# A two-layer trunk on one core: reordering the end of the attention, with 18 output-projection products inside it

## The chip, the cores and the metric

The kernel runs on one core of a Trainium2 chip. The metric is device time in microseconds (us) of one execution; a comparison takes medians of several executions.

## The reference

The model has two layers over 128 context tokens and 512 latent tokens of width 1024. Layer 0 is gated grouped-query attention (16 heads of 64, 4 key/value heads), layer 1 a gated linear recurrence in both directions (8 heads of 128). Each layer ends in a product with an output matrix, a gate and a LayerNorm. What the change touches is layer 0 from the softmax to its norm:

```python
s = jnp.einsum('bqkgd,bskd->bkgqs', q_blk, kf) * scale
p = jax.nn.softmax(s, axis=-1)
o = jnp.einsum('bkgqs,bskd->bqkgd', p, vf)
...
gated = o.reshape(B, L, ATTN_WIDTH) * jax.nn.silu(g)
out = gated @ w_out
x = _layer_norm(DEEPNORM_ALPHA * x + gate * out, ln_gain, ln_bias)
```

Latent tokens read the 128 cached context keys and all 512 latent keys; context tokens read the context alone.

## The kernel before, in words

All matrix products keep full precision by splitting each fp32 operand into a high and a low part (hi, lo) and adding three products: hi·hi, hi·lo, lo·hi. A weight piece of 128x1024 is loaded into a buffer `raw`, cast by ScalarE into its high part (L232), and VectorE subtracts to get the low part (L233). `raw` has three buffers, so a load for a later piece is issued by SyncE when VectorE has finished the subtraction of the piece three places before it. The order of the pieces is fixed: the eight pieces of the attention's output matrix (`in_attn_w_out`: four for output columns 0 to 511, `nh` = 0, then four for `nh` = 1), then those of the recurrence's input matrix (`in_rec_w_in`).

**Attention.** The work is a list of 36 units, nine for each of the four key/value heads (`att_gen`, L976). A sample unit is one head against 256 latent queries, as two blocks of 128. For each block there is a *front* (L927): four products of scores `sc` on TensorE (L838, L839), the row maximum on VectorE (`nm`, L932), the exponential on ScalarE (`p`, L935, with the row sum read out after it), the reciprocal on VectorE (`rc`, L939) and the scaling of the probabilities on GpSimd (`p`, L940). Then come ten transposes of the two blocks' probabilities (`pt`, L947) and their copies into SBUF (`pts`, L843: two by ScalarE, one by VectorE). Two heads make a pair, and when both are transposed the pair's value products follow (`pot`, L865; ten per pair, each of which the trace counts as two instructions); VectorE multiplies the result by the gate path (`gs`, L870). The code issues fronts two units ahead. All of this, with the projections of the next queries, stands in one block that is ordered by a scheduler (`first_half`, a simulated timeline); an instruction that is wrapped in `pin` keeps its place in program order on its engine. Before the change the scores, transposes and value products aren't pinned.

The gated output `gs` is split into `hhi` and `hlo` (L1063, L1064), eight column groups k = 0 to 7. The groups 0 to 5 belong to the first three key/value heads and are split while the last head is still at work; groups 6 and 7 are split at the end. The last four pieces of the output matrix (`nh` = 1) go into memory that the attention has used, so ScalarE can cast them only when the last value product is done.

**Output projection and norm, layer 0** (second block, from L1202). For each tile `tt` of 128 tokens and each `nh`, 24 products of 128x512 (three for each k) make `outp` (L1112 to L1114). VectorE multiplies by the gate, adds the scaled residual, and takes the statistics (L1128 to L1130, in `Norm.half`); after both `nh`, `Norm.finish` aggregates, GpSimd takes the power -1/2, and VectorE normalises `y` in two halves (L1141). The normalised tile is then transposed (`h1t`, L1208, in `h1_tile`) to become input of layer 1. The order is (tt, nh) = (0,0), (1,0), (0,1), (1,1), then the first transposes `h1t` of tile 0, then (2,0), (2,1), `h1t` of tile 1 and so on. Between the parts the first two pieces of `in_rec_w_in` are cast and subtracted (`rhi`, `rlo`).

**PSUM.** During the attention it is three pools: `b2` (two double banks, scores), `pop` (one bank, value products), `b1` (three banks, transposes and others). `Phase(4, 0)` replaces them by four double banks. Before the change it is opened inside the first block.

**Order on an engine.** Each engine runs its own instructions strictly in order; an instruction that waits holds all behind it on that engine.

Of the kernel before, what the change touches and what calls it, by code (L numbers as in the profile page):

```python
# [11 lines left out]
F32 = mybir.dt.float32  # L12
# [3 lines left out]
ALU = mybir.AluOpType  # L16
AX = mybir.AxisListType

P = 128
D = 1024  # L20
KT = D // P
# [3 lines left out]
CW = 256  # L25
NH = 16
NKV = 4
HD = 64
# [8 lines left out]
LEAD = (1, 1)  # L37
RAW_START = 8
EARLY = 2
WARM = (8, 2, 3)  # L40
D_SCALE = 2
D_OUTS = 2
# [83 lines left out]
def drain(gen):  # L126
    for _ in gen:
        pass
# [3 lines left out]
def hybrid_step(ctx: ExitStack, tc: tile.TileContext, a: dict, o: dict):  # L132
# [3 lines left out]
    def pool(name, bufs, **kw):  # L136
        return tc.tile_pool(name=name, bufs=bufs, **kw)
# [15 lines left out]
    class Phase:  # L153
        def __init__(self, n2, n1):
            self.st = ExitStack()
            if n2:
                pools["b2"] = self.st.enter_context(pool("b2", n2, space=PSUM))
            pools.pop("b1", None)
            if n1:
                pools["b1"] = self.st.enter_context(pool("b1", n1, space=PSUM))  # L160
# [673 lines left out]
                        next(att)  # L834


    def score_mms(out, X, c, h, t0, k0, k1):
        nc.tensor.matmul(out, X[:, h, t0:t0 + P], kk[:, c, k0:k1], start=True, stop=False)  # L838
        nc.tensor.matmul(out, X[:, h, t0:t0 + P], klo[:, c, k0:k1], start=False, stop=True)  # L839

    def keep_pt(ps, w, eng):
        t = sm.tile([P, w], F32, tag=f"pt{w}", name="pts", bufs={512: 6, 256: 4}[w])
# [11 lines left out]
    def tick():  # L854
        due = [f for f in later if f[0] <= 1]
        later[:] = [f for f in later if f[0] > 1]
        for f in later:
            f[0] -= 1
        for _, fn in due:
            fn()  # L860

    def av_mms(pot, slot, c, moving, first, last):

        for j in (1, 0):
            nc.tensor.matmul(pot[j * HD:(j + 1) * HD, :CW], vv[:, slot, c * HD:(c + 1) * HD], moving[j], start=first, stop=last)  # L865

    def av_out(pot, gt):
        tv = pot[:, :CW]
# [54 lines left out]
    def sample_unit(c, h, qh):  # L923
        j = h % 2
        ps, pts = {}, {}

        def front(i):  # L927
            sc = bank2("sc")
            for n, (k0, k1) in enumerate(HALVES):
                score_mms(sc[:, n, :320], Xs[c], c, h, (2 * qh + i) * P, k0, k1)  # L930
            nm = tiny.tile([P, 4], F32, tag="nm", name="nm")
            nc.vector.tensor_reduce(nm[:, 0:1], sc[:, :, :320], AX.XY, ALU.max, negate=True)  # L932
            p = ps[i] = prob_tile("p")
            su = tiny.tile([P, 4], F32, tag="su", name="su")
            nc.scalar.activation(halves(p[:]), sc[:, :, :320], AF.Exp, bias=nm[:, 0:1], accum_out=su[:, 0:1])  # L935

            def scale():
                rs = tiny.tile([P, 4], F32, tag="rc", name="rc")
                nc.vector.reciprocal(rs[:, 0:1], su[:, 0:1])  # L939
                nc.gpsimd.tensor_scalar(p, p, rs[:, 0:1], 1.0, ALU.mult, ALU.mult)  # L940
            defer(D_SCALE, scale)

        def trans(k0, m):
            pt = bank1("pt")
            for i in range(m):
                for q in range(2):
                    nc.tensor.transpose(pt[:, i * 256 + q * P:i * 256 + (q + 1) * P],  # L947
                                        ps[q][:, (k0 + i) * P:(k0 + i + 1) * P], ident)
            pts[k0] = keep_pt(pt, m * 256, nc.scalar.copy if m == 2 else nc.vector.tensor_copy)
            for i in range(m):  # L950
                live[j, k0 + i] = pts[k0][:, i * 256:(i + 1) * 256]

        def pair():
            mine = {k: live.pop(k) for k in list(live)}

            def apply():
                pot = pop[0].tile([P, 512], F32, tag="po", name="pot")
                for n, k in enumerate((4, 0, 1, 2, 3)):
                    av_mms(pot, k, c, [mine[0, k], mine[1, k]], n == 0, n == 4)
                av_out(pot, gs[:, 2 * c + h // 2, qh * 256:(qh + 1) * 256])  # L960
            return apply

        return (c, [lambda: front(0), lambda: front(1)], [lambda: trans(0, 2), lambda: trans(2, 2), lambda: trans(4, 1)],
                pair if j else None)

    def att_gen(side):
        units = []
        for c in range(4):
            units += [sample_unit(c, j, qh) for qh in range(2) for j in range(2)] + [prompt_unit(c)]
            units += [sample_unit(c, 2 + j, qh) for qh in range(2) for j in range(2)]  # L970
        AHEAD = 2

# [12 lines left out]
        for u in range(AHEAD):  # L985
            for f in fronts(u):
                run(f)
                yield
        pending = []

        def flush():
            while pending:
                run(pending.pop(0))
                yield

        for u, (c, _, back, end) in enumerate(units):
# [12 lines left out]
            back_of[0] = c  # L1009
            if end:  # L1010
                pending.append(end if len(back) == 2 else end())
        yield from flush()
        while later:
            tick()

    side = Side()
    att = att_gen(side)
# [32 lines left out]
        return modA, modB  # L1050

    wo = {}

    def wo_gen(layer, pieces, wpool):
        for nh, i in pieces:
# [36 lines left out]
    right.close()  # L1092


    ph = Phase(4, 0)
    h1p = rpool("h1p", 1)
    h1lo = h1p.tile([P, KT, NT], F32R, tag="h1lo", name="h1lo")
    wr = rpool("wr", 2)
# [8 lines left out]
    def out_mms(ps, tt, nh, ghi, glo, ks=range(KT), c=slice(0, 512)):  # L1107
        t = slice(tt * P, (tt + 1) * P)
        out = bank_of(ps, nh, c)
        for k in ks:  # L1110
            hi, lo = (w[:, k % 2, c] for w in wo[nh, k // 2])
            nc.tensor.matmul(out, ghi[:, k, t], hi, start=(k == 0), stop=False)  # L1112
            nc.tensor.matmul(out, ghi[:, k, t], lo, start=False, stop=False)  # L1113
            nc.tensor.matmul(out, glo[:, k, t], hi, start=False, stop=(k == KT - 1))  # L1114

    class Norm:
# [7 lines left out]
        def half(self, nh):  # L1124
            s = slice(nh * 512, (nh + 1) * 512)
            y = self.y[:, s]
            g = gate[0][:, 1 if self.tt == TS else 0, s]
            nc.vector.tensor_tensor(y, self.ps[:, nh, :], g, ALU.mult)  # L1128
            nc.vector.scalar_tensor_tensor(y, self.x[:, s], ALPHA, y, ALU.mult, ALU.add)
            nc.vector.bn_stats(self.st[:, nh, :], y)  # L1130

# [68 lines left out]
    drain(split_gs(range(6, 8)))  # L1200
    drain(wo_gen(0, PIECES[4:], wob))
    first_half.__exit__(None, None, None)  # L1202
    h1hi = gsp.tile([P, KT, NT], F32R, tag="gs", name="h1hi")
    def h1_tile(tt, y):
        s = 1 if tt == TS else 0
        pt = bank2("h1t")
        for ft in range(KT):
            nc.tensor.transpose(pt[:, ft // 4, (ft % 4) * P:(ft % 4 + 1) * P], y[:, ft * P:(ft + 1) * P], ident)  # L1208
        t = slice(tt * P, (tt + 1) * P)
        for nh in range(2):  # L1210
            h = lnp.tile([P, 512], F32, tag="h", name="h1", bufs=2)
            for f in range(4):
                ft = 4 * nh + f
                src, dst = pt[:, nh, f * P:(f + 1) * P], h[:, f * P:(f + 1) * P]
                ma, mb = modA[:, ft, s:s + 1], modB[:, ft, s:s + 1]
                if f % 2:
                    nc.scalar.activation(dst, src, AF.Identity, bias=mb, scale=ma)
                else:
                    nc.vector.tensor_scalar(dst, src, ma, mb, ALU.mult, ALU.add)
            f = slice(4 * nh, 4 * nh + 4)  # L1220
            split_act(h1hi[:, f, t], h1lo[:, f, t], h[:].rearrange("p (a b) -> p a b", a=4))
# [116 lines left out]
    first = proj_gen(0, H, True)  # L1338
    next(first)
    norms = {}  # L1340
    for tt, nh in ((0, 0), (1, 0), (0, 1), (1, 1), (2, 0), (2, 1), (3, 0), (3, 1), (4, 0), (4, 1)):
        if nh == 0:
            norms[tt] = Norm(tt)
        out_mms(norms[tt].ps, tt, nh, hhi, hlo)
        norms[tt].half(nh)
        if nh == 1:
            norms[tt].finish()
            if tt > 1:
                h1_tile(tt - 1, norms[tt - 1].y)
            elif tt == 1:  # L1350
                h1_tile(0, norms[0].y)
    for _ in range(4):
        next(first)
    h1_tile(TS, norms[TS].y)
# [373 lines left out]
```

## Time and profile before

| | |
|---|---|
| median of 3 runs | 844.93 us (841.62 to 847.22) |
| the profiled execution | 845.85 us, of which the span of the profile is 844.1 us |
| TensorE busy | 817.6 us, 97% of the span |
| VectorE, ScalarE, GpSimd busy | 531.3, 383.3, 211.5 us |
| mean granted clock of TensorE | 0.989 |
| last value product of the attention ends | 337.2 us |
| first output-projection product starts | 337.73 us |
| first transposes `h1t` start | 359.67 us |

A row of the timeline reads: start, duration, engine, line and operation, out<-in and shape, count, and in brackets how long the engine had been idle before it and what ended that. A matmul's listed duration overlaps the next one's; the pace is the distance between starts. PEclk is the clock that TensorE was granted, as a share of full speed. In a chain row the number is the time that the chain spends there.

### The profile page before, as it was taken

How to read it: one execution, taken by the hardware profiler on the slowest of the kernel's cores; microseconds unless marked ns; L12 is line 12 of the kernel's file. 1: busy time of each engine (PE TensorE's matmuls, PEld its weight loads, DVE VectorE, ACT ScalarE, POOL GpSimd, SP SyncE). 2: the span in 40 equal slices, each digit the busy share in tenths (PEclk: the TensorE clock that was granted, in tenths of full speed). 3: DMA queues.
4: the chain of work that ended last, by engine and by line, in shares of the span. 5: the costliest groups of instructions: out<-in, count | busy, mean ns of one | idle time of the engine just before them, and what ended most of it. 6: DMA issues, size and time to landing. Idle time of an engine off the chain costs nothing.

```text
span 844.1 us, 19415 instructions
## 1 busy us (share of the span) xinstructions
PE 817.6 (97%) x8157; PEld 732.2 (87%) x8157; DVE 531.3 (63%) x954; ACT 383.3 (45%) x771; POOL 211.5 (25%) x263
## 2 busy tenths in 40 slices
PE   8999998999999998999999999999999999999994
PEld 6789998878789765888999999999999999998774
DVE  4566434675756665776438575767668575858476
ACT  2242536474756765322434434445434544445232
POOL 0123002343334752110001304143333314121121
PEclk9999999999999999999999999999999999999997
DMA  9932212144151153631322322331422322324041
GB/s 333 384 114 76 78 49 77 51 142 166 54 203 51 51 200 101 218 131 36 106 71 63 106 73 84 83 108 52 107 89 83 91 68 89 120 64 158 21 162 75
DMA packets 34134, 92.50 MB, mean 110 GB/s; under 512 B 5040, under 2 KB 12224, under 8 KB 34048
## 3 DMA queue, kind: packets, MB, share of 16 engines
q1 hardware_dynamic: 23280, 73.05, 25.8%
q0 software_dynamic: 4864, 14.44, 5.8%
q10 hardware_dynamic: 5904, 3.78, 1.5%
q8 instruction: 64, 1.05, 0.5%
q14 instruction: 22, 0.18, 0.1%
HBM read 82.06 MB, written 9.19 MB: 108 GB/s over the span
## 4 chain that ended last, share of the span: by engine, by line
PE 88%; DVE 5%; ACT 2%; DMA 2%; issue 1%; POOL 0%; SPq 0%; DVEq 0%; ACTq 0%; POOLq 0%
PE rps L1273 7%; PE rps L1274 7%; PE rps L1275 7%; PE vgps L1263 5%; PE vgps L1265 5%; PE vgps L1264 5%; PE pot L865 4%; PE outp L1112 4%; PE pt L947 3%; PE outp L1114 3%; PE outp L1113 3%; PE acc L523 3%; PE lv L1406 2%; PE gps L338 2%; PE gps L339 2%; PE sc L838 2%
## 5 line engine op out<-in xcount | busy, mean ns | idle before, releaser
L1273 PE MATMUL rps<-h1hi,rhi 128*128 128x320 f32 x368 | 118.3, 321 | 0.0
L1274 PE MATMUL rps<-h1lo,rhi 128*128 128x320 f32 x368 | 113.8, 309 | 0.0
L1275 PE MATMUL rps<-h1hi,rlo 128*128 128x320 f32 x368 | 113.6, 309 | 0.0
L940 POOL TENSOR_SCALAR p<-p,rc 128x640 f32<-128x640 f32 x64 | 54.1, 847 | 124.7 <-DVE rc L939 108.7
L932 DVE TENSOR_REDUCE nm<-sc 128x1 f32<-128x640 f32 x64 | 52.1, 819 | 33.6 <-PE sc L839 33.0
L1273 PEld LDWEIGHTS rps<-h1hi,rhi 128*128 128x128 f32 x368 | 69.1, 188 | 1.3
L1274 PEld LDWEIGHTS rps<-h1lo,rhi 128*128 128x128 f32 x368 | 69.2, 188 | 0.0
L1275 PEld LDWEIGHTS rps<-h1hi,rlo 128*128 128x128 f32 x368 | 69.1, 188 | 0.0
L233 DVE TENSOR_TENSOR rlo<-raw,rhi 128x1024 fp32r<-128x1024 f32 x32 | 45.0, 1407 | 34.1 <-ACT rhi L232 34.0
L1434 POOL COPY At<-near 32x160 f32<-32x160 f32 x32 | 14.0, 438 | 196.0 <-DVE near L1396 195.0
L935 ACT ACTIVATE p<-sc,nm 128x640 f32<-128x640 f32 x64 | 51.3, 803 | 23.3 <-DVE nm L932 12.9
L232 ACT CAST rhi<-raw 128x1024 fp32r<-128x1024 f32 x32 | 33.6, 1048 | 52.7 <-PE rps L1274 49.2
L1384 ACT COPY kc<-A 128x640 f32<-128x640 f32 x40 | 32.3, 806 | 54.4 <-DVE A L1415 50.7
L947 PE MATMUL pt<-small,p 128*128 128x128 f32 x320 | 49.8, 280 | 2.7 <-POOL p L940 1.7
L1263 PE MATMUL vgps<-rhi,h1hi 128*128 128x256 f32 x180 | 51.5, 286 | 0.0
L1264 PE MATMUL vgps<-rlo,h1hi 128*128 128x256 f32 x180 | 50.9, 283 | 0.0
L1265 PE MATMUL vgps<-rhi,h1lo 128*128 128x256 f32 x180 | 50.8, 282 | 0.0
L843 ACT COPY pts<-pt 128x512 f32<-128x512 f32 x64 | 36.0, 589 | 28.4 <-PE pt L947 28.0
L947 PEld LDWEIGHTS pt<-small,p 128*128 128x128 f32 x320 | 37.4, 142 | 11.6 <-issue 6.0
L838 PE MATMUL sc<-kk,X 128*128 128x320 f32 x128 | 43.0, 345 | 3.0 <-ACT p L935 2.8
L1263 PE MATMUL vgps<-wspare,h1hi 128*128 128x256 f32 x140 | 41.7, 298 | 0.0
L865 PE MATMUL pot<-pts,vv 128*64 128x256 f32 x320 | 40.4, 398 | 1.1 <-DVE pts L843 1.1
(299 smaller groups left out, 2394.2 us busy)
## 6 DMA issues: line engine op xcount, KB each, us to landing
raw<-in_rec_w_in SPq DMA_DIRECT2D x40, 512.0 KB, 3.6
raw<-in_ada_s SPq DMA_DIRECT2D x32, 512.0 KB, 4.1
raw<-in_ada_m SPq DMA_DIRECT2D x16, 512.0 KB, 8.0
raw<-in_attn_w_in SPq DMA_DIRECT2D x16, 512.0 KB, 4.4
raw<-in_attn_w_out SPq DMA_DIRECT2D x8, 512.0 KB, 3.8
raw<-in_rec_w_out SPq DMA_DIRECT2D x8, 512.0 KB, 3.6
x1d<-y SPq DMA_DIRECT2D x5, 512.0 KB, 2.6
rx<-x1d POOLq DMA_DIRECT2D x20, 128.0 KB, 3.2
```

The costliest lines, as they stand in the source:

```text
L838: nc.tensor.matmul(out, X[:, h, t0:t0 + P], kk[:, c, k0:k1], start=True, stop=False)
L865: nc.tensor.matmul(pot[j * HD:(j + 1) * HD, :CW], vv[:, slot, c * HD:(c + 1) * HD], moving[j], start=first, stop=last)
L932: nc.vector.tensor_reduce(nm[:, 0:1], sc[:, :, :320], AX.XY, ALU.max, negate=True)
L935: nc.scalar.activation(halves(p[:]), sc[:, :, :320], AF.Exp, bias=nm[:, 0:1], accum_out=su[:, 0:1])
L940: nc.gpsimd.tensor_scalar(p, p, rs[:, 0:1], 1.0, ALU.mult, ALU.mult)
L947: nc.tensor.transpose(pt[:, i * 256 + q * P:i * 256 + (q + 1) * P], ps[q][:, (k0 + i) * P:(k0 + i + 1) * P], ident)
L1263: nc.tensor.matmul(out, h1hi[:, k, t], hi, start=(k == 0), stop=False)
L1264: nc.tensor.matmul(out, h1hi[:, k, t], lo, start=False, stop=False)
L1265: nc.tensor.matmul(out, h1lo[:, k, t], hi, start=False, stop=(k == KT - 1))
L1273: nc.tensor.matmul(ps[:, j, :320], hi[:, k, :], h1hi[:, k, t], start=(k == 0), stop=False)
L1274: nc.tensor.matmul(ps[:, j, :320], hi[:, k, :], h1lo[:, k, t], start=False, stop=False)
L1275: nc.tensor.matmul(ps[:, j, :320], lo[:, k, :], h1hi[:, k, t], start=False, stop=(k == KT - 1))
```

## The change

It has four parts.

1. From the third unit before the end on, the scores, transposes and value products are pinned (`listed_pe`), so TensorE takes them in program order. Ahead of the last unit but one, the pair's value products are flushed from the queue before that unit's transposes are written, so the last unit's scores come ahead of them.
2. 18 products of the output projection, tile 0, `nh` = 0, k = 0 to 5, move from the second block into this order, as `outq` in the `b2` pool: 6 after the last unit but one, 4 after the last unit's transposes, 8 after the last value products. ScalarE then copies them out in two halves (`part`). In the second block tile 0 computes k = 6 and 7 alone (6 products), and VectorE adds the two halves of `part` before the gate; the gate product then reads SBUF.
3. The second block starts with tile 1: (1,0), (0,0), (1,1), (0,1), and the first transposes `h1t` are those of tile 1.
4. `Phase(4, 0)` is opened in the second block, and its `b2` pool is given `reuse_waits="tile"`: a tile waits for the earlier users of its own banks, and not for all of the closed pools.

```diff
+EARLY_OUT = (6, 4, 8)
...
-                pools["b2"] = self.st.enter_context(pool("b2", n2, space=PSUM))
+                pools["b2"] = self.st.enter_context(pool("b2", n2, space=PSUM, reuse_waits="tile"))
...
+    def listed_pe(ins):
+        return pin(ins) if listed[0] else ins
...
         for u, (c, _, back, end) in enumerate(units):
             fr = fronts(u + AHEAD)
+            left_over = len(units) - u
+            if left_over == 3:
+                listed[0] = True
+            if left_over == 2:
+                yield from flush()
             for n, b in enumerate(back):
...
+            if left_over < 3:
+                early_out(EARLY_OUT[2 - left_over])
+                yield
         yield from flush()
         while later:
             tick()
+        early_out(EARLY_OUT[2])
+        drain(early)
...
+    def early_mms():
+        ps = bank2("outq")[:, 0, :]
+        t = slice(0, P)
+        for k in range(6):
+            hi, lo = (w[:, k % 2, :] for w in wo[0, k // 2])
+            for x, w in ((hhi, hi), (hhi, lo), (hlo, hi)):
+                yield pin(nc.tensor.matmul(ps, x[:, k, t], w, start=(k == 0 and x is hhi and w is hi),
+                                           stop=(k == 5 and x is hlo)))
+        for n in range(2):
+            part.append(rowp.tile([P, CW], F32, tag="row", name="part"))
+            nc.scalar.copy(part[n], ps[:, n * CW:(n + 1) * CW])
...
+    def early_out(n):
+        side.finish()
+        for _ in range(n):
+            next(early)
...
-            nc.vector.tensor_tensor(y, self.ps[:, nh, :], g, ALU.mult)
+            if (self.tt, nh) == (0, 0):
+                for n in range(2):
+                    c = slice(n * CW, (n + 1) * CW)
+                    nc.vector.tensor_tensor(y[:, c], self.ps[:, 0, c], part[n], ALU.add)
+                nc.vector.tensor_tensor(y, y, g, ALU.mult)
+            else:
+                nc.vector.tensor_tensor(y, self.ps[:, nh, :], g, ALU.mult)
...
-    for tt, nh in ((0, 0), (1, 0), (0, 1), (1, 1), (2, 0), (2, 1), (3, 0), (3, 1), (4, 0), (4, 1)):
+    for tt, nh in ((1, 0), (0, 0), (1, 1), (0, 1), (2, 0), (2, 1), (3, 0), (3, 1), (4, 0), (4, 1)):
...
-        out_mms(norms[tt].ps, tt, nh, hhi, hlo)
+        if (tt, nh) == (0, 0):
+            out_mms(norms[tt].ps, tt, nh, hhi, hlo, range(6, KT), first=6)
+        else:
+            out_mms(norms[tt].ps, tt, nh, hhi, hlo)
```

The move of `ph = Phase(4, 0)` behind the end of the first block, the wrapping of four matmul calls in `listed_pe` and the order of the later `h1_tile` calls are left out of the diff above.

What the scheduler makes of it shows in the order of the instructions on an engine. First TensorE at the end of the attention, before the change, from the value products of the last pair but one to those of the last pair (`pot` value products, `pt` transposes, `sc` scores):

```order
L865 MATMUL pot<-pts,vv 64x256 x10
L947 MATMUL pt<-small,p 128x128 x3
L838 MATMUL sc<-kk,X_2860 128x320
L839 MATMUL sc<-klo,X_2860 128x320
L838 MATMUL sc<-kk,X_2860 128x320
L839 MATMUL sc<-klo,X_2860 128x320
L947 MATMUL pt<-small,p 128x128 x17
L865 MATMUL pot<-pts,vv 64x256 x10
```

The same stretch with the change, from the second half of the last scores on to the first of the four products that follow the last transposes; behind its last row stand three more `outq`, the ten last `pot` and eight `outq`:

```order
L844 MATMUL sc<-kk,X_2860 128x320
L845 MATMUL sc<-klo,X_2860 128x320
L871 MATMUL pot<-pts,vv 64x256 x10
L954 MATMUL pt<-small,p 128x128 x10
L1079 MATMUL outq<-wohi,hhi 128x512
L1079 MATMUL outq<-wolo,hhi 128x512
L1079 MATMUL outq<-wohi,hlo 128x512
L1079 MATMUL outq<-wohi,hhi 128x512
L1079 MATMUL outq<-wolo,hhi 128x512
L1079 MATMUL outq<-wohi,hlo 128x512
L954 MATMUL pt<-small,p 128x128 x10
L1079 MATMUL outq<-wohi,hhi 128x512
```

The last scores moved ahead of the value products of the pair before, and six products now stand between the transposes of the last two units, four ahead of the last value products.

Second, VectorE from the last gate product of the attention into the second block, before the change (`wolo` low parts of the output matrix, `rlo` low parts of `in_rec_w_in`; the branch is the border of the blocks):

```order
L870 TENSOR_TENSOR gs<-pot,gs 128x256
L233 TENSOR_TENSOR wolo<-raw,wohi 128x1024 x2
L1064 TENSOR_TENSOR hlo<-gs,hhi 128x640
L233 TENSOR_TENSOR wolo<-raw,wohi 128x1024 x2
L1202 UNCONDITIONAL_BRANCH
L1128 TENSOR_TENSOR y<-outp,gate_105 128x512
L1129 TENSOR_SCALAR y<-x,y 128x512
L233 TENSOR_TENSOR rlo<-raw,rhi 128x1024 x2
L1130 BN_STATS st<-y 128x6
L1128 TENSOR_TENSOR y<-outp,gate_105 128x512
```

The same stretch with the change:

```order
L234 TENSOR_TENSOR wolo<-raw,wohi 128x1024 x2
L1102 TENSOR_TENSOR hlo<-gs,hhi 128x640
L234 TENSOR_TENSOR wolo<-raw,wohi 128x1024 x2
L1245 UNCONDITIONAL_BRANCH
L234 TENSOR_TENSOR rlo<-raw,rhi 128x1024 x2
L1171 TENSOR_TENSOR y<-outp,gate_105 128x512
L1172 TENSOR_SCALAR y<-x,y 128x512
L1168 TENSOR_TENSOR y<-outp,part 128x256
L1173 BN_STATS st<-y 128x6
L1168 TENSOR_TENSOR y<-outp,part 128x256
L1169 TENSOR_TENSOR y<-y,gate_105 128x512
L1172 TENSOR_SCALAR y<-x,y 128x512
```

The two subtractions of `rlo` moved ahead of the first work on an `outp`, and two additions of `part` came in.

More of the change, by code (lines that the diff above doesn't have):

```diff
@@ L864, in av_mms @@
         for j in (1, 0):
-            nc.tensor.matmul(pot[j * HD:(j + 1) * HD, :CW], vv[:, slot, c * HD:(c + 1) * HD], moving[j], start=first, stop=last)
+            listed_pe(nc.tensor.matmul(pot[j * HD:(j + 1) * HD, :CW], vv[:, slot, c * HD:(c + 1) * HD], moving[j],
+                                       start=first, stop=last))
     def av_out(pot, gt):
@@ L1014, in att_gen @@
             tick()
+        early_out(EARLY_OUT[2])
+        drain(early)
+        listed[0] = False
     side = Side()
@@ L1105, in bank_of, with out_mms @@
         return ps[nh, c.start][:, 0, c] if isinstance(ps, dict) else ps[:, nh, c]
-    def out_mms(ps, tt, nh, ghi, glo, ks=range(KT), c=slice(0, 512)):
+    def out_mms(ps, tt, nh, ghi, glo, ks=range(KT), c=slice(0, 512), first=0):
         t = slice(tt * P, (tt + 1) * P)
@@ L1111, in out_mms @@
             hi, lo = (w[:, k % 2, c] for w in wo[nh, k // 2])
-            nc.tensor.matmul(out, ghi[:, k, t], hi, start=(k == 0), stop=False)
+            nc.tensor.matmul(out, ghi[:, k, t], hi, start=(k == first), stop=False)
             nc.tensor.matmul(out, ghi[:, k, t], lo, start=False, stop=False)
```

20 lines of the change are left out of this document (11 added, 9 removed).

## Prediction, made before the changed kernel was run

> **What bounds the kernel now.** I read the page's chain of waits first, then TensorE's timeline at the end of the attention, then the queues of ScalarE, VectorE and SyncE behind it. The chain's shares by engine say that TensorE sets nearly all of the time, so a gain has to come from time in which it stands still or runs slowly:
>
> ```profile
> PE 88%; DVE 5%; ACT 2%; DMA 2%; issue 1%; POOL 0%; SPq 0%; DVEq 0%; ACTq 0%; POOLq 0%
> ```
>
> TensorE's rows of the last 13 us of the attention (idle time and what ended it in brackets):
>
> ```profile
> 324.69 2.38 PE L865 MATMUL pot<-pts,vv 128*64 128x256 f32 x20 [0.63 <-DVE pts L843]
> ...
> 327.30 0.39 PE L838 MATMUL sc<-kk,X 128*128 128x320 f32 x1
> ...
> 329.22 0.72 PE L947 MATMUL pt<-small,p 128*128 128x128 f32 x3 [0.33 <-ACT pts L843]
> 331.63 0.98 PE L947 MATMUL pt<-small,p 128*128 128x128 f32 x7 [1.69 <-POOL p L940]
> 333.13 4.07 PE L865 MATMUL pot<-pts,vv 128*64 128x256 f32 x20 [0.52 <-DVE pts L843]
> 337.73 0.50 PE L1112 MATMUL outp<-wohi,hhi 128*128 128x512 f32 x1 [0.53 <-DVE gs L870]
> ```
>
> Nothing else is left to run there: the last scores start at 327.30, and their softmax passes through VectorE, ScalarE and GpSimd while TensorE waits 1.69 us. The waits from there on sum to 3.07 us. The last value products take 4.07 us besides. At full clock a pair takes 2.31 us and ten transposes 1.09 us, as two chain rows from a busy stretch show:
>
> ```profile
> 291.14 1.09 PE pt L947 x10
> ...
> 292.82 2.31 PE pot L865 x20
> ```
>
> That difference of 1.76 us is the clock, as TensorE's busy time and granted clock by stretches show (length, busy, count, clock, DMA):
>
> ```profile
> 135.00:137.00 2.00, 0.09 (x1) 1.00 0.72 236
> 139.00:140.00 1.00, 1.00 (x6) 0.50 0.32 94
> 330.00:332.00 2.00, 0.37 (x3) 1.00 0.00 0
> 334.00:335.00 1.00, 1.00 (x8) 0.50 0.00 0
> 787.00:788.00 1.00, 0.16 (x5) 1.00 0.00 0
> 788.00:792.00 4.00, 4.00 (x39) 1.00 0.00 0
> ```
>
> Two stretches of 2 us with little work are each followed, some 2 us later, by half clock; after a gap of under 1 us at 787 the clock stays. So a long gap costs itself and about 1.76 us more.
>
> **The change, part by part.** *The last scores ahead of the value products.* Their buffer is free when ScalarE has finished the exponential before last:
>
> ```profile
> 324.33 0.80 ACT L935 ACTIVATE p<-sc,nm 128x640 f32<-128x640 f32 x1
> 325.03 0.20 ACT L935 ACTIVATION_READ_ACCUMULATOR p<-sc,nm 128x1 f32 x1
> ...
> 328.49 1.07 ACT L843 COPY pts<-pt 128x512 f32<-128x512 f32 x2 [1.40 <-PE pt L947]
> 329.45 0.81 ACT L935 ACTIVATE p<-sc,nm 128x640 f32<-128x640 f32 x1
> ```
>
> That is at 325.23, so they start at 325.25 and not at 327.30, 2.05 us sooner. The last exponential also no longer stands behind the two copies of 328.49. I put the last scaled probabilities at about 329.3; before, the transposes that wait for them start at 331.63. TensorE then goes on from 326.25 (an estimate: the reduction and the copy that VectorE does ahead of the value products) with work that stands ready: value products to 328.56, ten transposes to 329.65, six `outq`, ten transposes to 332.1, four `outq` to 333.0, value products to 335.35, eight `outq` to 337.2. An `outq` costs 0.2285 us, the pace of the 96 products between the first `outp` at 337.73 above and the first `h1t`:
>
> ```profile
> 359.43 0.39 PE L1114 MATMUL outp<-wohi,hlo 128*128 128x512 f32 x1
> 359.67 1.03 PE L1208 MATMUL h1t<-small,y 128*128 128x128 f32 x8
> ```
>
> (359.67 - 337.73) / 96 = 0.2285. The six hide VectorE's and ScalarE's copies of the transposes, the four hide VectorE's last copy. The last value products would end 1.85 us sooner (337.20 to 335.35). Bounds: if the last scores gain nothing, 337.20; if no small gap stays at all, about 334.4.
>
> *18 products moved.* TensorE ends `outq` at 337.2 with 18 x 0.2285 = 4.11 us of the projection done, where before it had none at 337.73: a lead of 4.11 + 0.53 = 4.64 us.
>
> *PSUM pool and branch.* The 0.53 us for `gs` is gone, since `outp` waits only for TensorE's own older work. What a border of two blocks costs an engine that doesn't wait there can be seen on VectorE below: it passes from the last `wolo` to the first `y` without a gap, so I take nothing. If TensorE paid up to 0.53 us, the next wait would swallow it.
>
> *Tile 1 first.* TensorE has 78 of the 96 products left before the first `h1t`: 78 x 0.2285 = 17.8 us, so it stands there at 355.0, 4.64 us sooner. Is VectorE as fast? Its queue before:
>
> ```profile
> 345.86 1.23 DVE L233 TENSOR_TENSOR wolo<-raw,wohi 128x1024 fp32r<-128x1024 f32 x1 [3.18 <-ACT wohi L232]
> 347.00 0.68 DVE L1128 TENSOR_TENSOR y<-outp,gate 128x512 f32<-128x512 f32 x1
> 347.72 0.69 DVE L1129 SCALAR_TENSOR_TENSOR y<-x,y 128x512 f32<-128x512 f32 x1
> 348.33 2.35 DVE L233 TENSOR_TENSOR rlo<-raw,rhi 128x1024 fp32r<-128x1024 f32 x2
> 350.60 0.69 DVE L1130 BATCH_NORM_STATS2 st<-y 128x6 f32<-128x512 f32 x1
> ...
> 354.42 0.69 DVE L1128 TENSOR_TENSOR y<-outp,gate 128x512 f32<-128x512 f32 x1 [1.09 <-PE outp L1114]
> ...
> 357.71 1.00 DVE L1141 TENSOR_SCALAR y<-y,mv,rstdl 128x512 f32<-128x512 f32 x2 [0.71 <-POOL rstdl L189]
> ```
>
> Before, the first half of `y` was normalised at 357.71 + 0.50 = 358.21, 1.46 us ahead of `h1t`. That slack is smaller than the lead of 4.64. And with the change both `rlo` stand ahead of the first `y`, so all of the norm hangs on the second piece of `in_rec_w_in`. Its transfer hangs on `raw` buffers, in ScalarE's and SyncE's rows:
>
> ```profile
> 337.37 2.00 ACT L232 CAST wohi<-raw 128x1024 fp32r<-128x1024 f32 x2 [4.02 <-PE pot L865]
> 339.27 0.73 ACT L1063 CAST hhi<-gs 128x640 fp32r<-128x640 f32 x1
> 339.90 1.04 ACT L232 CAST wohi<-raw 128x1024 fp32r<-128x1024 f32 x1
> ...
> 346.67 1.06 ACT L232 CAST rhi<-raw 128x1024 fp32r<-128x1024 f32 x1 [0.85 <-DMA raw<-in_rec_w_in]
> 347.95 1.06 ACT L232 CAST rhi<-raw 128x1024 fp32r<-128x1024 f32 x1 [0.22 <-DMA raw<-in_rec_w_in]
> ```
>
> ```profile
> 340.83 2.20 SPq L213 DMA_DIRECT2D raw<-in_rec_w_in  x2
> ```
>
> The casts wait for the last value product, so the whole row moves 1.85 us forward. The third `wohi` now also waits behind the two copies of `part`, of the shape of a copy that takes 0.39 us in the lead-in:
>
> ```profile
> L777 ACT COPY vv<-acc x3: 361/391/420, 55.8 to 57.4; 128x256 f32<-128x256 f32 x3
> L327 DVE TENSOR_TENSOR acc<-acc,adaps x16: 396/412/422, 142.0 to 312.4; 128x256 f32<-128x256 f32 x16
> ```
>
> Third `wohi` from 339.90 - 1.85 + 0.78 = 338.83 to 339.87, its subtraction (1.23) to 341.1. Then the second piece is issued, where before it was issued at 340.83 + 2.20 - 0.33 = 342.70. It took 347.95 - 342.70 = 5.25 us until its cast started; with the same 5.25 that is 346.35, the cast (1.06) ends at 347.4, `rlo` (half of 2.35) at 348.6; before, it was 350.68. From there VectorE does y, residual, addition, statistics, addition, gate, residual, statistics: six steps of about 0.66 (four steps took from 350.68 to 354.42 - 1.09 = 353.33) and two additions of 0.41 (the row of L327 above) make 4.8; then the second half of tile 1 up to the normalised half, 354.42 to 358.21, 3.79. It is ready at 348.6 + 8.6 = 357.2.
>
> So `h1t` starts at 357.2 and not at 355.0: 2.2 us of the lead become a wait. The gain at this point is 359.67 - 357.2 = 2.45. Bounds of the transfer: the page's median landing for these pieces and, at the other end, no earlier arrival than before (347.95):
>
> ```profile
> raw<-in_rec_w_in SPq DMA_DIRECT2D x40, 512.0 KB, 3.6
> ```
>
> With 3.6 us it lands at 344.7, the cast ends at 346.05 behind the first piece's, `rlo` at 347.3, `h1t` starts at 355.9. With 347.95 `rlo` ends at 350.2 and `h1t` starts at 358.8. I take 5.25, the row of this very transfer, whose neighbours (two loads of `x`, two other pieces) move with it.
>
> *The clock.* The old gap of 1.69 us and its half clock are gone (already in 335.35). The new gap of 2.2 us is longer than the two that were followed by half clock, so I charge 1.76 us for it, on the projection's products, which TensorE alone bounds afterwards.
>
> *Other edits.* The last four output-matrix pieces are needed sooner: the last one's subtraction would end at about 345.25 (347.09 - 1.85), TensorE reads it at 337.2 + 48 x 0.2285 = 348.2; hidden with 2.9 us to spare. The two additions and the gate from SBUF are in the 4.8. Pins cost nothing by themselves.
>
> Sum: -4.64 + 2.2 + 1.76, about -0.7 us. Against the profiled execution's own 845.85 (span 844.1 and 1.75 around it) that is 845.15. This execution lies 0.92 above the median shown, so the median goes from 844.93 to 844.2.
>
> **The rivals.** *The gap leaves the clock alone.* The gain is then 2.45 us, 842.5. [...] Against it: 2.2 us is longer than 1.69. [...]
>
> *The transfers come sooner.* With 3.6 us to landing the gap is 0.9 us, the clock stays as at 787, and the gain is 3.8: 841.1. For it: most pieces land so fast. Against it: here they took 5 us and more beside the loads of `x`, and these move along.
>
> *Slower: the second recurrent piece comes no sooner.* If DMA, not the issue, sets its arrival, it comes at 347.95, `h1t` starts at 358.8 after a gap of 3.8 us, and with the clock's 1.76 the sum is -0.87 + 1.76 = +0.9: 845.8. It decides from a start of `h1t` later than 357.9, that is an arrival after 347.1. To be slower by 1% it would have to come some 7 us later than that; nothing in the queue is that late.
>
> *Nothing gained from the order:* if the last scores don't move forward, the attention ends as before with 10 products inside; VectorE's row stands still, the same as the slower case.
>
> **How the numbers follow.** Gap and clock 0.40, gap without clock 0.23, transfers sooner 0.15, slower 0.15, something else 0.07. The likeliest gives 844.2. The range takes in the cases from 841.1 to 845.8, and half a us on each side for the median of runs that spread from 841.62 to 847.22: 840.6 to 846.3. One per cent (8.4 us) is about what a measurement of this kernel can tell from no change; the largest gain, the whole lead with no gap, is 4.64, and no slower case reaches 8.4. Faster by over 1% 0.02, within 1% 0.94, slower by over 1% 0.04.
>
> **What would show it.** In the profile after: the last scores about 2 us sooner against the value products around them, no wait over 1 us ahead of the last value products, and those at 2.3 us. No wait at the first `outp`. Both `rlo` directly ahead of the first `y`, and TensorE waiting about 2 us for VectorE's `y` ahead of the first `h1t`, with the clock at 0.5 for some 3.4 us after it. I am wrong if that `h1t` doesn't wait (then the gain is near 4.6), if the last value products still run at half clock, or if TensorE waits for `wohi` or `hhi` in the second block.

## The result and the profile after

| | before | after |
|---|---|---|
| median of 17 runs each | 845.18 us | 847.97 us |
| ratio after / before | | 1.0026, 95% interval 1.0015 to 1.0037 |
| profiled execution, its span | 845.85, 844.1 us | 845.34, 843.2 us |
| outside the span | 1.75 us | 2.14 us |

The change makes the kernel slower by some 2.2 us (0.0026 x 845). The forecast was 0.7 us faster, in a range that ended at 846.3. The profiled execution of after is the shortest of its 17, and that of before holds two stretches of half clock that it was spared: at 139 the row of before, shown in the prediction, has 0.50; after has

```profile
139.00:140.00 1.00, 1.00 (x11) 1.00 0.74 303
```

So spans can't be compared as they are. I measure both from one common event: the first product of the last unit's scores (its first block of 128; the "last scores" of the prediction are its second block). In the timeline of before that row is

```profile
323.23 0.40 PE L838 MATMUL sc<-kk,X 128*128 128x320 f32 x1
```

and the first `h1t` at 359.67 comes 36.44 us behind it. TensorE's rows after, from the same event on:

```profile
320.56 0.39 PE L844 MATMUL sc<-kk,X 128*128 128x320 f32 x1
...
322.60 0.41 PE L844 MATMUL sc<-kk,X 128*128 128x320 f32 x1 [0.99 <-ACT p L942]
...
330.44 2.38 PE L871 MATMUL pot<-pts,vv 128*64 128x256 f32 x20
...
334.69 0.39 PE L1149 MATMUL outp<-wohi,hhi 128*128 128x512 f32 x1
...
341.26 0.39 PE L1151 MATMUL outp<-wohi,hlo 128*128 128x512 f32 x1
346.05 0.59 PE L1149 MATMUL outp<-wohi,hhi 128*128 128x512 f32 x1 [4.40 <-DVE y L1171]
...
358.69 1.03 PE L1252 MATMUL h1t<-small,y 128*128 128x128 f32 x8
```

To `h1t` it is now 38.13 us, 1.69 more. The event is not quite free of the change: of the ten transposes that stood ahead of it, two now stand behind it. From `potp`, the last row up to which TensorE's order is unchanged (319.99 before, 317.17 after), it is 1.84 us more. Over the runs below, the event lies 3.02 to 3.39 us behind that row, so differences of 0.2 or 0.3 us between two runs mean little. What follows is equal: from the first `h1t` to the end of the span 484.4 us before, 484.5 after. With the 0.39 us more outside the span that is 2.1 us, and the ratio's interval, 1.3 to 3.1 us, holds it.

The gain came: the first `outp` of the second block starts 14.13 us behind the common event with 18 products done, against 14.50 with none, which is a lead of 0.37 + 18 x 0.2285 = 4.48 us. Then TensorE stands still for 4.40 us ahead of the first product of part (1,1), the third of the block. VectorE's rows say why:

```profile
341.24 1.23 DVE L234 TENSOR_TENSOR wolo<-raw,wohi 128x1024 fp32r<-128x1024 f32 x1 [2.88 <-ACT wohi L233]
342.88 2.51 DVE L234 TENSOR_TENSOR rlo<-raw,rhi 128x1024 fp32r<-128x1024 f32 x2 [0.42 <-ACT rhi L233]
345.31 0.68 DVE L1171 TENSOR_TENSOR y<-outp,gate 128x512 f32<-128x512 f32 x1
```

The last of these reads part (1,0) out of PSUM. Parts (1,0) and (1,1) are the two banks of one PSUM tile, and the write to the second bank, at 346.05, waits until the read of the first is over, at 345.31 + 0.68 = 345.99. The read stands behind both `rlo`, as the order showed before the run, and these end at 345.39; VectorE is idle for 0.42 us ahead of them, though the last product of (1,0) started at 339.90. The page's chain of waits follows the same way back, through the transfer of the second piece of `in_rec_w_in`:

```profile
338.38 4.69 DMA raw<-in_rec_w_in
343.09 1.05 ACT rhi L233
344.31 1.00 issue
345.31 0.69 DVE y L1171
346.05 0.59 PE outp L1149
```

Behind the gap the clock is halved for 3.4 us, and products come 0.43 us apart instead of 0.23 (length, busy, count, clock, DMA):

```profile
345.00:346.00 1.00, 0.00 (x0) 1.00 1.05 238
346.00:347.00 1.00, 0.95 (x3) 0.66 0.54 152
347.00:348.00 1.00, 1.00 (x4) 0.50 0.92 365
348.00:349.00 1.00, 1.00 (x4) 0.50 0.99 406
349.00:350.00 1.00, 1.00 (x4) 0.63 0.28 102
350.00:351.00 1.00, 1.00 (x6) 1.00 0.00 0
```

The 48 products to `h1t` take 358.69 - 346.05 = 12.64 us instead of 48 x 0.2285 = 10.97, that is 1.67 us. The sum, -4.48 + 4.40 + 1.67 = +1.59, leaves 0.1 of the 1.69 open.

### The profile page after: what moved, and what is told of

The parts are those of the page before. It is cut to its first block, busy times and chain, and to the rows that moved or that the text cites. A ratio compares the mean times of both kernels' runs of the same rounds, so it can differ in the third digit from the quotient of the medians.

```text
span 843.2 us, 19423 instructions
## 1 busy us (share of the span) xinstructions
PE 814.0 (97%) x8157; PEld 729.5 (87%) x8157; DVE 532.3 (63%) x956; ACT 383.8 (46%) x773; POOL 211.2 (25%) x263
## 4 chain that ended last, share of the span: by engine, by line
PE 86%; DVE 6%; DMA 4%; ACT 2%; issue 2%; POOL 0%; SPq 0%; DVEq 0%; ACTq 0%; POOLq 0%
PE rps L1317 7%; PE rps L1318 7%; PE rps L1319 7%; PE vgps L1307 5%; PE vgps L1309 5%; PE vgps L1308 5%; PE pot L871 4%; PE pt L954 4%; PE outp L1149 3%; PE outp L1150 3%; PE outp L1151 3%; PE lv L1452 2%; PE acc L524 2%; PE gps L339 2%; PE gps L340 2%; PE gps L341 2%
## 5 line engine op out<-in xcount | busy, mean ns | idle before, releaser
L339 PE MATMUL gps<-hhi,whi 128*128 128x320 f32 x128 | 40.0, 313 | 0.4 <-ACT X L692 0.4
```

The costliest lines, as they stand in the source:

```text
L339: nc.tensor.matmul(ps[:, :320], w.hi(k)[:, c], hhi[:, k, t], start=(k == 0), stop=False)
```

## The experiments

Theory W: the loss is TensorE's wait for VectorE's read of the other half of the same PSUM tile, a read that stands behind `rlo`, and the half clock after it. Rival D: the weights of `nh` = 1 come too late for the earlier products. Rival C: the attention itself or its clock. The table gives what each run measured: time from the common event to the first `h1t`, TensorE's waits ahead of the third part of the block and ahead of `h1t` in the profiled execution, and the ratio to the kernel before. Each ratio is against runs of the kernel before on the same chip and at the same time; the median beside it is that run's own. The times to `h1t` come from one execution each; half clock elsewhere and the time outside the span count in the ratio alone, so the two columns can differ by 1 or 2 us.

| run | to `h1t`, us | wait third part | wait `h1t` | median, us | ratio |
|---|---|---|---|---|---|
| before | 36.44 | 0 | 0 | 845.18 | 1 |
| after | 38.13 | 4.40 | 0 | 847.97 | 1.0026 (1.0015 to 1.0037) |
| halves split | 33.43 | 0 | 1.45 | 843.01 | 0.9979 (0.9966 to 0.9991) |
| `rlo` later | 34.67 | 2.54 | 0 | 844.69 | 0.9999 (0.9985 to 1.0014) |
| both | 33.01 | 0 | 0.94 | 842.64 | 0.9977 (0.9961 to 0.9992) |
| both, `rlo` last | 31.85 | 0 | 0 | 840.89 | 0.9957 (0.9941 to 0.9973) |
| order alone | 33.27 | 0 | 0 | 841.55 | 0.9966 (0.9953 to 0.9979) |
| order and pool | 32.68 | 0 | 0 | 841.43 | 0.9966 (0.9951 to 0.9982) |
| no moved products | 32.68 | 0 | 0 | 840.59 | 0.9948 (0.9930 to 0.9965) |
| tile 0 first | 34.47 | 0.81 | 0 | 842.07 | 0.9972 (0.9958 to 0.9986) |
| 19 spare products | 36.82 | 0.37 | 0 | 847.89 | 1.0026 (1.0010 to 1.0042) |
| 14 spare products | 37.12 | 1.80 | 0 | 847.25 | 1.0025 (1.0009 to 1.0041) |
| after, repeated | | | | 849.73 | 1.0050 (1.0034 to 1.0066) |
| after, second execution | 38.97 | 4.36 | 0 | 848.38 | 1.0022 (1.0000 to 1.0044) |

**Halves split.** The two halves of `outp` of tiles 0 and 1 get PSUM tiles of their own, which the four double banks have room for:

```diff
-            self.tt, self.ps = tt, bank2("outp")
+            self.tt, self.ps = tt, {(nh, 0): bank2("outp") for nh in range(2)} if tt < 2 else bank2("outp")
```

> The changed kernel with one edit: in tiles 0 and 1 the two column halves of outp lie in PSUM tiles of their own, so the products of (1,1) no longer wait for VectorE's read of (1,0). Theory W (the loss is TensorE's wait of 4.4 us for that read, which stands behind both rlo, and the half clock of 1.76 us after it): no wait before (1,1); VectorE's queue is as before, so the norm of tile 1 comes late and a shorter wait of about 1.5 us appears at the first h1t; 3 to 5 us faster than the changed kernel, 1 to 3 us faster than the kernel before (ratio 0.997 to 0.999). Theory D (those products wait for their weights of nh = 1): the wait of over 4 us stays, ratio about 1.003. Theory C (the loss lies in the attention or in the clock's phase): ratio about 1.003.

The wait ahead of (1,1) is gone, though VectorE reads (1,0) as late as before (345.54), and with the wait the half clock. That shows the tile to be the cause, and rules out D: the same weights are used 4.4 us sooner without a wait. What is left appears where the prediction had put all of it, ahead of `h1t`. TensorE's row:

```profile
354.17 1.11 PE L1252 MATMUL h1t<-small,y 128*128 128x128 f32 x8 [1.45 <-DVE y L1184]
```

**`rlo` later.** The two subtractions follow tile 1's first two steps, and the PSUM tiles stay as they are:

```diff
-    next(first)
...
         added = norms[tt].half(nh)
+        if (tt, nh) == (1, 0):
+            hold.append(added.ins)
+            next(first)
+            hold.clear()
```

> The changed kernel with one edit: VectorE's two rlo stand behind the first two steps on tile 1 and its first addition, where the kernel before had them, and not ahead of them. Theory W: VectorE reads outp of (1,0) right after its last wolo, some 2.8 us sooner; the wait before (1,1) falls from 4.4 to about 1.6 us, the clock may stay up, no wait at h1t: about 4 us faster than the changed kernel, 2 us faster than the kernel before (ratio about 0.997). Theory D: the wait stays at 4 us, ratio 1.003. If only the clock were to blame, the wait would stay.

The wait shrinks from 4.40 to 2.54, not to 1.6. VectorE's row of the last `wolo` shows the difference:

```profile
344.41 1.23 DVE L234 TENSOR_TENSOR wolo<-raw,wohi 128x1024 fp32r<-128x1024 f32 x1 [3.95 <-ACT wohi L233]
345.55 0.68 DVE L1171 TENSOR_TENSOR y<-outp,gate 128x512 f32<-128x512 f32 x1
```

The last value products end here at 334.84 (332.53 + 2.31), so the last `wolo` starts 9.57 us behind them; after, 341.24 - 332.75 = 8.49. The piece's landing differs by 1.1 us between executions. Without that 1.1 us the wait would be near 1.5, as expected; `rlo` and the transfer it waits for make the other 3 us.

**Both**, and then **both with `rlo` behind tile 1's normalised `y`** (the subtractions held by the second normalising instruction instead of the first residual):

> Both edits together: outp halves of tiles 0 and 1 in PSUM tiles of their own, and rlo behind the first steps on tile 1. Theory W: no wait before (1,1) and none at h1t, the whole lead of 4.5 us stays: ratio about 0.995. My recorded step that VectorE's norm of tile 1 is late for the first h1t by about 2 us: that wait would show here too if it doesn't hang on rlo. Theory D: ratio about 1.003.

> The changed kernel with the halves of outp of tiles 0 and 1 in PSUM tiles of their own, and both rlo behind tile 1's normalised y (in the run with both edits they stood between its first steps). Theory W (what is left of the loss there, 0.94 us ahead of the first h1t, is VectorE's rlo ahead of the norm): h1t doesn't wait, 32.1 us behind the first row of the last scores instead of 33.01, median about 841.7, ratio 0.9966. Rival (VectorE's norm is bound by the last wolo and its load, or later pieces of in_rec_w_in come too late and TensorE waits behind the projection): 33 us or a new wait later, median 842.6 or more.

The first leaves 0.94 us at `h1t`, where none was expected; the second none. VectorE's rows of the first show the reason: from the last `wolo` to the norm's statistics it has no idle time, and `rlo` takes 2.4 us there.

```profile
344.05 0.68 DVE L1171 TENSOR_TENSOR y<-outp,gate 128x512 f32<-128x512 f32 x1
344.77 0.69 DVE L1172 SCALAR_TENSOR_TENSOR y<-x,y 128x512 f32<-128x512 f32 x1
345.38 1.22 DVE L234 TENSOR_TENSOR rlo<-raw,rhi 128x1024 fp32r<-128x1024 f32 x1
346.51 0.69 DVE L1173 BATCH_NORM_STATS2 st<-y 128x6 f32<-128x512 f32 x1
347.12 1.21 DVE L234 TENSOR_TENSOR rlo<-raw,rhi 128x1024 fp32r<-128x1024 f32 x1
```

With both edits and `rlo` last, the whole lead arrives: 36.44 - 31.85 = 4.59 us.

**Order alone.** Part 1 of the change on the kernel before: scores, transposes and value products pinned and flushed, no moved product, tile 0 first, the pool as before. The first lines of the edit (the others take back parts 3 and 4):

```diff
-EARLY_OUT = (6, 4, 8)
+EARLY_OUT = (0, 0, 0)
...
-        drain(early)
```

> The kernel before with part 1 of the change alone: last scores ahead of the value products and TensorE's order pinned from the third unit before the end; no products moved, tiles and PSUM pools as before. By the trace of the changed kernel, TensorE would end the attention some 10.5 us after the start of the last scores but one, against 13.97 us before; that is 3.5 us faster (ratio 0.996), most of it the waits of 0.3 to 1.7 us and the half clock of 1.76 us at the last value products. Rival: the products are what fills the wait, and without them the wait for the last softmax and the half clock stay: ratio about 1.000.

It gives 3.17 us up to `h1t`, near the 3.5 expected, and rules out C: the attention gains. Its value products run at full clock behind a small wait, and the wait for `gs` is still there:

```profile
329.09 2.38 PE L871 MATMUL pot<-pts,vv 128*64 128x256 f32 x20 [0.52 <-DVE pts L849]
332.00 0.50 PE L1149 MATMUL outp<-wohi,hhi 128*128 128x512 f32 x1 [0.53 <-DVE gs L877]
```

**Order and pool.** The same with `Phase(4, 0)` in the second block and its waits by tile (part 4):

> The new order of scores, transposes and value products alone, as in the run of that part by itself, and besides Phase(4, 0) opened in the second block with reuse_waits='tile'; no products moved, tile 0 first. Theory: the 0.53 us in which TensorE waited for gs ahead of the first outp goes, so the first h1t comes 32.7 us behind the first row of the last scores instead of 33.27; the time outside the span is 2.1 us if the later pool makes it so, 1.75 if not; median 841.0 to 841.4, ratio 0.996. Rival (the border of two blocks or the pool costs TensorE as much as it gives): 33.3 us and 841.9.

To `h1t` 32.68, as expected: the border of two blocks costs TensorE nothing, and 0.59 us are won. The medians of the two can't be told apart.

**No moved products**: the changed kernel without part 2, so with tile 1 first.

> The changed kernel without its 18 moved products: the new order, the pool in the second block, and tile 1 first. Theory W (the wait needs both: few products ahead of (1,1) and rlo ahead of the first y): VectorE's queue is that of the kernel before with the first y ahead of rlo, 48 products (11 us) cover its read, TensorE doesn't wait ahead of (1,1), first h1t 32.7 us behind the first row of the last scores, median 841.4, ratio 0.9966. Rival (the order of the tiles by itself brings the wait): over 1 us ahead of (1,1), median above 842.5.

32.68 again and no wait. VectorE reads (1,0) from 342.06 to 342.74 (behind the last `wolo` alone: `rlo` stands behind the first steps here), and TensorE comes to (1,1) at 343.21:

```profile
343.21 0.39 PE L1148 MATMUL outp<-wohi,hhi 128*128 128x512 f32 x1
```

So 48 products in front cover the read with half a microsecond to spare, as long as `rlo` stands behind it. With 30 and the same order on VectorE ("`rlo` later") there is a hole of 2.54 us. Why the scheduler sets `rlo` ahead of that read when the 18 products are moved, and not otherwise, wasn't tried.

**Tile 0 first**: the changed kernel without part 3.

> The changed kernel with the second block's order as before the change: (0,0), (1,0), (0,1), (1,1), first h1t of tile 0. TensorE meets the products of k = 7 at once, so it waits some 1.3 us for hlo in (0,0), but VectorE has the two additions of tile 0 right behind the last wolo and ahead of rlo. Theory W (the loss is the wait for a PSUM read that stands behind rlo): the third part (0,1) waits under 0.7 us, no half clock, first h1t about 34 us behind the first row of the last scores, median about 843.2, ratio 0.998. Rival (18 products sooner simply outrun the pieces of nh = 1, whatever the order): the wait ahead of the third part stays at 3 us or more, with a half clock behind it, median about 847.

TensorE's two waits, for `hlo` of k = 7 and ahead of the third part, and VectorE's order:

```profile
339.72 0.50 PE L1151 MATMUL outp<-wohi,hlo 128*128 128x512 f32 x1 [0.82 <-DVE hlo L1102]
346.48 0.50 PE L1149 MATMUL outp<-wohi,hhi 128*128 128x512 f32 x1 [0.81 <-DVE y L1168]
```

```profile
345.68 0.75 DVE L1168 TENSOR_TENSOR y<-outp,part 128x256 f32<-128x256 f32 x2
...
348.52 2.34 DVE L234 TENSOR_TENSOR rlo<-raw,rhi 128x1024 fp32r<-128x1024 f32 x2
```

As Theory W has it: the read comes ahead of `rlo`, and the wait is 0.81 instead of 4.40. With the new order, the moved products without the swap and the swap without them are both faster than before; the two together are slower.

**Spare products.** Products that write a PSUM tile that nobody reads fill TensorE's gap, so that the price of the half clock can be seen apart from the wait:

```diff
             out_mms(norms[tt].ps, tt, nh, hhi, hlo, range(6, KT), first=6)
+            spare = bank2("spare")
+            for _ in range(19):
+                nc.tensor.matmul(spare[:, 0, :], hhi[:, 0, :P], wo[0, 0][0][:, 0, :], start=True, stop=True)
```

> The changed kernel with 19 extra products of 128x512 behind the six of tile 0, written to a PSUM tile that nobody reads, so that TensorE works through the 4.40 us in which it waited (19 x 0.2285 = 4.34). Theory W (the half clock after the gap comes from the gap): the first product of (1,1) starts as late as before, but the clock stays at 1.00 behind it, so the first h1t comes 1.76 us sooner, 36.4 us behind the first row of the last scores instead of 38.13; median about 846.2, ratio to the kernel before about 1.001. Rival (the clock falls at that place for another reason, such as the time since the last fall): half clock as in the changed kernel, 38.1 us, median about 848.

In the profile the clock stays at 1.00 behind the fill, and `h1t` comes 1.31 us sooner than after. But its median is that of after, which ran at another time. So 14 spare products ran in turn with the changed kernel, and a second execution of the changed kernel was profiled:

> As the run with 19 extra products that nobody reads, but with 14 (3.2 us), so that TensorE is through with them about 1.2 us before VectorE's read is done and nothing is late for them. Theory W (the half clock comes from the gap of 4.40 us): a gap near 1.2 us, no half clock, first h1t 36.4 us behind the first row of the last scores, and over the runs 1.2 to 1.8 us less than the changed kernel in this batch. Rival (the clock's fall in the profiled execution isn't the rule, or the fill costs as much elsewhere): less than 0.7 us below the changed kernel, as the medians of the run with 19 suggest (847.89 against 847.97).

> The changed kernel itself once more, on the same chip and in turn with the next two, so that a difference of 1 to 2 us can be told. Median 847.5 to 848.3, ratio 1.002 to 1.004; a wait near 4.4 us ahead of the first product of (1,1) and half clock for some 3.4 us behind it.

> A second profiled execution of the changed kernel, because the first one is the shortest of its 17 executions (845.34 against a median of 847.97). Theory W: the wait ahead of (1,1) is again 4 us or more and a half clock of some 3.4 us follows; what makes the usual execution longer lies ahead of the last scores (falls of the clock near 10 and 140 us that the first one was spared) or in a longer wait for VectorE, up to 5 us. Rival: the wait is much shorter, under 3 us, and the time is lost at a place that the first profile doesn't show.

Side by side the 14 lie (1.0050 - 1.0025) x 845 = 2.1 us below the changed kernel, though their intervals just overlap, with no half clock behind a gap of 1.80 us. Of that repeat only the times are used. In the profile the gain to `h1t` is 1.01, since (1,1) starts 26.08 us behind the common event and not 25.49. The changed kernel itself has ratios from 1.0022 to 1.0050, so the price of the half clock over many runs stays open between nothing and some 2 us. That the fill keeps the clock up is not an accident of the profiled executions: the mean granted clock is 0.9932 over the 12 executions of either kernel with spare products, 0.9891 over the 11 of the repeat and 0.9907 over the 17 of after. (The kernel before has 0.990 to 0.991 in every set of runs for which it is on record.) A difference of 0.0041 over 846 us is 6.9 us less at half clock (0.0041 x 846 / 0.5), one of 0.0025 is 4.2. In the profiles the price is plain. The second execution pays more of it than the first:

```profile
350.43 0.80 PE L1149 MATMUL outp<-wohi,hhi 128*128 128x512 f32 x1 [4.36 <-DVE y L1171]
```

```profile
347.00:348.00 1.00, 0.00 (x0) 1.00 0.01 0
348.00:349.00 1.00, 0.00 (x0) 0.80 0.74 139
...
351.00:352.00 1.00, 1.00 (x4) 0.50 0.84 307
...
355.00:356.00 1.00, 1.00 (x5) 0.79 0.00 0
356.00:357.00 1.00, 1.00 (x6) 1.00 0.00 0
```

The wait is the same to 0.04 us, but the clock falls inside the gap and is back only at 355.4: 48 products take 363.76 - 350.43 = 13.33 us, 2.36 over full clock. To `h1t` it is 2.53 us more than before.

## Why the prediction was wrong, step by step

- **The last scores 2.05 us sooner: right.** They start 4.07 us behind the common event before (327.30 - 323.23) and 2.04 after (322.60 - 320.56).
- **The last value products end 1.85 us sooner, at full clock: right.** 13.97 us behind the common event before, 330.44 + 2.31 - 320.56 = 12.19 after, 1.78 sooner.
- **A lead of 4.64 us from the 18 products and the `gs` wait: right,** 4.48, and no wait at the first `outp`.
- **`rlo` ends at 348.6, 25.4 us behind the common event: right,** 24.8 (345.39 - 320.56); the transfer of the second piece took 4.69 from its release, not 5.25.
- **"So `h1t` starts at 357.2 and not at 355.0: 2.2 us of the lead become a wait": this step, *Tile 1 first*, failed.** It had VectorE's lateness right and took the norm ahead of `h1t` for the first thing that waits for it. The PSUM read stands in the same queue some 8 us ahead of that, and (1,1) needs it. By the forecast's own numbers TensorE gets to (1,1) at 337.2 + 30 x 0.2285 = 344.06, and the read is over at 348.6 + 0.68 = 349.3: a wait of 5.2 us instead of 2.2. It measured 4.40, and `h1t` didn't wait. The prediction took an `h1t` that doesn't wait for the sign of a gain near 4.6; the whole lead was lost ahead of it. The rows of before had the slack: there the read of (0,0) is over at 347.68 (the row of 347.00 in the prediction), and TensorE comes to part (0,1) at 348.78, 1.1 us later. The change takes 4.5 us from that and puts `rlo` ahead of the read. Further on the same wait shows in small, when a weight load ahead of part (2,1) comes 0.27 us late for the read of (2,0):

```profile
348.78 0.39 PE L1112 MATMUL outp<-wohi,hhi 128*128 128x512 f32 x1
```

```profile
367.06 0.19 PEld L1112 LDWEIGHTS outp<-wohi,hhi 128*128 128x128 f32 x1 [0.27 <-DVE y L1128]
```

- **1.76 us for the clock: right in size, by luck.** It measured 1.67 here and 2.36 in the second execution, but behind gaps of 4.4 us, and the term was charged for one of 2.2. Gaps of that length mostly left the clock alone: 2.54 us ("`rlo` later") and 1.80 us (14 spare products) did. The gap near 136 us, one of the two that the prediction took its rule from, is there with 2.12 us in all 13 profiled executions that this document uses. In three of them half clock follows it (before, order and pool, the second execution of after), in ten it doesn't. Its row before, where half clock follows, and after, where it doesn't:

```profile
137.21 0.41 PE L838 MATMUL sc<-kk,X 128*128 128x320 f32 x1 [2.12 <-ACT p L935]
```

```profile
135.58 0.41 PE L844 MATMUL sc<-kk,X 128*128 128x320 f32 x1 [2.12 <-ACT p L942]
```

- **The rival in which a gap leaves the clock alone** was refuted for a gap of 4.4 us alone; for the 2.2 us that it was written for, these counts are on its side.
- **The slower rival named another mechanism.** It had the second piece come no sooner; it came sooner, and the sign turned for the PSUM tile.
- **0.39 us outside the span** was not in the sum. It belongs to the kernel and not to one execution: the mean is 2.1 us outside the span over the runs of after and of every kernel with moved products but one, and 1.8 over those of before, of the three kernels without moved products, and of both with `rlo` last. The later pool doesn't make it (order and pool: 1.8); what does is open.

So the terms -4.64, +2.2 and +1.76 should have been -4.48, +4.40 and +1.67, a loss of 1.6 us up to `h1t` instead of a gain of 0.7. What the change has to give lies in its parts 1 and 4, 3.76 us to `h1t`. The moved products add 0.83 us to that at best (32.68 to 31.85), since TensorE has to do them in any case, and they take away the cover under which VectorE read PSUM.

## What to carry to other kernels

When work is moved out of a stretch, list what that work covered: every wait on the same engine whose releaser doesn't move along, in order of time, and the PSUM reads that free a tile for its next writer first of all. Take the queue of the releasing engine row by row and stop at the first row that someone waits for, not at the last. If two halves of a PSUM tile are written at different times, give them tiles of their own (4.40 us of wait after, none with the halves split), or keep the read of the first half ahead of other work on its engine.

## What the runs showed of the hardware

In these traces half clock comes in pieces of one length. A share of 0.66 in a slice of 1 us means half clock for 0.68 us of it; read so, it lasts from 346.32 to 349.74 after (3.42 us), from 333.52 to 336.94 before (3.42), and from 348.60 to 355.42 in the second execution of after (6.82, twice that). Gaps of 4.40 and 4.36 us, equal but for where these pieces begin, cost 1.67 and 2.36 us.

The pieces also begin on a grid. The falls of the clock at 9.26, 138.96, 333.52 and 835.28 before are 129.70, 194.56 and 501.76 us apart, those at 346.32 and 834.42 after 488.10, and those at 140.38 and 348.60 in the second execution of after 208.22. 129.70 / 38, 194.56 / 57, 501.76 / 147, 488.10 / 143 and 208.22 / 61 all give 3.413, the length of one piece as far as slices of 1 us tell; half clock from 835.28 and from 834.42 on lasts to the end of the span. Where the grid lies differs between executions, and with it how much of a wait falls into one step. Before, 1.66 us of the wait of 2.12 lie in the step from 135.55 to 138.96, and half clock follows. After, the grid carried back from the fall at 346.32 cuts the same wait at 134.70, into 1.24 and 0.88 us, and the clock stays. Over the 13 executions, each with the grid from a fall of its own, one step holds 1.66 to 1.98 us of this wait in the three with half clock behind it, and at most 1.58 in the ten others. The gap of 1.69 us at the end of the attention shares its step, 330.11 to 333.52, with the wait of 0.52 us behind it, 2.04 us of standing in all. The wait of 2.54 us ("`rlo` later") is cut into 0.94 and 1.60, by the grid from a fall at 10.19 in that execution, and the clock stayed. Idle time in a step doesn't settle it, though: with 14 spare products the wait of 1.80 us lies in one step (345.56 to 348.97, by the grid from a fall at 11.05), and the clock stayed.

In the second execution the step that begins with the fall at 348.60 begins with 1.83 us of waiting (to 350.43), and half clock lasts for two pieces; after, the step that begins at 346.32 holds no wait, and it lasts for one. That the waiting makes the second piece was not shown.
